# Hybrid decoder block: gates as dot products, a second broadcast of silu(c), new places for four pieces of work

## The chip, the cores and the metric

One core of a Trainium2 chip runs the whole block. The metric is the device time of one execution in microseconds (us). A run's time is a little more than the span of its trace, which goes from the first to the last instruction.

## What is computed

The reference, cut to what the change touches (x is 512 x 1024, c is one row of 1024):

```python
mod = silu(c) @ w_ada + b_ada                      # 6 sections of 1024
shift1, scale1, gate1, shift2, scale2, gate2 = split(mod, 6)
h = rms_norm(x, norm1_g) * (1 + scale1) + shift1
z = h @ w_in                                       # u, v, q, k, v, indexer, gates
merged = sigmoid(g_a) * (gmlp(z) @ w_proj_a) + sigmoid(g_b) * (sparse_attention(z) @ w_proj_b)
x = x + gate1 * (merged @ w_out)
h2 = rms_norm(x, norm2_g) * (1 + scale2) + shift2
f_g, f_u = split(h2 @ w_ffn_in, 2)
x = x + gate2 * ((silu(f_g) * f_u) @ w_ffn_out)
out = rms_norm(x, final_norm_g)
```

## The kernel before, in words

All values are float32. A large product is taken in three matmuls, hi x hi, lo x hi and hi x lo, where hi is the rounded copy of an operand and lo the rest (helper lines 107 to 109). Weights come in chunks of 512 KB over SyncE's (SP's) queue, a stream with a fixed order (`ensure`, `prep`); ScalarE (ACT) makes hi (L161), VectorE (DVE) or GpSimd (POOL) makes lo (L165). Every engine runs its instructions in the order in which the program issues them; nothing is reordered.

**The head.** The four tiles of x (128 rows each) are loaded. ACT squares each and sums (L521), POOL turns the sum into 1/rms (L404, L405), DVE or ACT scales the tile (L525, L528). c arrives as a row; TensorE (PE) spreads it over 128 partitions in PSUM, as a matmul of a row of ones with c (L517, two matmuls of 512 columns), and ACT writes silu of it to `csb` (L533). The shift and scale of the first modulation are dot products along the row: `mod_row` lets DVE multiply 128 rows of the transposed weights `w_shsc` with csb and sum them into one column of G1 (L245). Then, for each of eight blocks of 128 columns (kt), PE transposes four tiles of x (L500), ACT applies scale and shift and writes hT (L505) and a full copy (L507), DVE takes the rest (L560), and PE makes 18 matmuls into two banks of k and four of q (L568, L570, L574). While PE waits in the head it multiplies the identity with itself (`keep_warm`, L513); the result isn't read. A chain of small DVE operations prepares the rotary angles (`run_chain`, L416 to L428), some of them ahead of the scalings, some within the kt loop.

**The gates.** gate1 and gate2 are made another way: `mod_sec` multiplies 16 chunks of w_ada with single values of silu(c) and adds them up on DVE (L234), with rows spread over the partitions; `sec_tasks` then sums over the partitions by two matmuls with ones into a bank named mod (L480, L481), and DVE adds that to the bias, which POOL's queue had broadcast (L483). For gate2 this stands at the end of q = 10 in the loop described next, in banks 3 and 2.

**The FFN's first products.** They run as a loop over q = 0 to 17, by a scheme that makes a 2 x 2 block of products out of seven smaller ones: seven times `sprod` into banks R[0] to R[3], where ACT copies one bank to seed the next (L1709, L1720), and the work of the following q (`pre[0]` to `pre[3]`) is issued in between.

**The end.** The last products are added to the residual by DVE (L1266, L1268), the last partial sum of squares is taken by a dot (L1908), POOL takes the power -1/2 (L1911), and `finish` scales the columns with ACT and DVE (L1776, L1777) and stores them.

A pool's tiles of one name share `bufs` buffers; a new tile of that name waits until the readers of the one that had the buffer are done.

Of the kernel before, what the change touches and what calls it, by code (L numbers as in the profile page):

```python
# [9 lines left out]
F32 = mybir.dt.float32  # L10
# [20 lines left out]
def _plan():  # L31
# [4 lines left out]
    def pairs(*starts):  # L36
# [10 lines left out]
        "w_ada": [(2 * q, 2, ((sec * D + 512 * h, 512),)) for sec in (2, 5) for h in range(2) for q in range(4)],  # L47
# [3 lines left out]
def _pack(w, name):  # L51
    import numpy as np
    rows = w.reshape(128, 8, -1).transpose(1, 0, 2) if name == "w_ada" else w.reshape(-1, 128, w.shape[1])
# [6 lines left out]
def block_kernel(ctx: ExitStack, tc: tile.TileContext, x, w_ada, b_ada, w_in,  # L60
# [7 lines left out]
    psum = ctx.enter_context(tc.tile_pool(name="psum", bufs=1, space=bass.MemoryType.PSUM))  # L68
# [3 lines left out]
    def packed(ap, name):  # L72
        at, o = {}, 0
        for k0, nk, cols_ in _plan()[name]:
# [5 lines left out]
    w_ada, w_in, w_ffn_in, w_ffn_out = (packed(*a) for a in ((w_ada, "w_ada"), (w_in, "w_in"), (w_ffn_in, "w_ffn_in"),  # L80
                                                             (w_ffn_out, "w_ffn_out")))
# [14 lines left out]
    def bank(k, name="bank"):  # L96
        return psum.tile([128, 512], F32, name=name, tag=f"b{k}", bufs=1)
# [101 lines left out]
    cols = tiny.tile([128, 64], F32, name="cols")  # L199
    cs = cols[:, 0:8]  # L200
# [9 lines left out]
    pack = mid.tile([128, 315], F32, name="pack", tag="A2", bufs=1)  # L210
    A.dma_start(pack, small)
# [15 lines left out]

    def mac(o, w, j, first, on_act=False):
        if first and on_act:
            A.activation(o, w, AF.Copy, scale=cs[:, j:j + 1])  # L230
        elif first:
            V.tensor_scalar(o, w, cs[:, j:j + 1], None, op0=OP.mult)
        else:
            V.scalar_tensor_tensor(o, w, cs[:, j:j + 1], o, op0=OP.mult, op1=OP.add)  # L234

    def mod_row(s, kt):
        k = slice(kt, kt + 1)
        o = G1[:, s, k] if s < 2 else Gc[:, 1, 8 * (3 - s) + kt:8 * (3 - s) + kt + 1]
        scale, init = ((1.0, bsh1), (n1c[:, k], bsc1), (1.0, bsh2), (n2c[:, k], bsc2))[s]
# [9 lines left out]
    acc = {}  # L249

    def mod_sec(sec):
        for half in range(2):
            for q in range(4):
                def dma(raw, half=half, q=q):
                    SY.dma_start(raw, w_ada(2 * q, 2, ((sec * D + half * 512, 512),)))

                def fn(raw, half=half, q=q):
                    if q == 0:
                        acc[sec, half] = base.tile([128, 512], F32, name="acc", tag="acc", bufs=2)
                    v = raw.rearrange("p (j n) -> p j n", j=2)  # L260
                    for j in range(2):
                        mac(acc[sec, half], v[:, j], 2 * q + j, q == 0 and j == 0)
                    if q == 3:
                        ah = None
                        if sec == 5:
                            return
                        if sec == 2:
                            ah = t512("ah", F32R)
                            al = base.tile([128, 512], F32R, name="al", tag="acc", bufs=2)
                            V.tensor_copy(ah, acc[sec, half])  # L270
                            V.tensor_sub(al, acc[sec, half], f(ah))
                            acc[sec, half] = al
                        sec_done.append((sec, half, tick[0] + 2, ah))
                yield dma, fn
# [23 lines left out]
    def mods_mid():  # L298
        yield from mod_sec(2)
        for s in (2, 3):  # L300
            for kt in range(8):
                yield mod_row(s, kt)
# [9 lines left out]
    stream[W_GB[1][0]]["lo"] = V  # L312
    W_PB = [group(w_pb, 256 * g, mods=mm_, nm=((0, 1), (1, 1), (1, 0), (0, 0))[g], mraw="k_hi") for g in range(4)]
# [3 lines left out]
    mg = mod_sec(5)  # L317
    wh = ["E5", "E6", "E0", "E1"]
# [74 lines left out]
    mhalf = tiny.tile([128, 8], F32, name="mhalf")  # L393
    ones = mid.tile([128, 128], F32, name="ones", tag="A3", bufs=1)
    onesr = tiny.tile([128, 128], F32R, name="onesr")
    P.memset(mhalf, -0.5)
# [71 lines left out]
    def sec_tasks(flush=False, one=False):  # L468
        tick[0] += 1
        while sec_done:  # L470
            if one and one == 2:
                break
            one = one and 2
            sec, half, t, ah = sec_done[0]
            if t >= tick[0] and not flush:
                break
            sec_done.pop(0)
            a = acc[sec, half]
            p = bank(mbank[0], "mod")
# [1490 lines left out]
```

## Time and profile before

| | us |
|---|---|
| median of 3 runs | 795.21 (794.40 to 795.68) |
| the profiled execution's own time | 796.31 |
| its span | 794.5 |
| PE busy | 782.0 |
| DVE busy | 679.9 |
| ACT busy | 424.6 |
| POOL busy | 162.3 |
| mean DMA rate | 177 GB/s |

The profiled execution is a single one, so its lines are read against its own time. Busy time of matmuls is modelled at their ends; start times are not. A row of the timeline has the start, the duration, the engine, the line, and behind the operation the idle time before it with what ended it; xN groups N instructions, and the duration is then that from the first start to the last end.

### The profile page before, as it was taken

The numbers are of one execution on the slowest core, as the hardware profiler recorded it, in microseconds if no ns is written. First come the engines' busy times: TensorE is split into PE (matmuls) and PEld (weight loads), VectorE is DVE, ScalarE is ACT, GpSimd is POOL, SyncE is SP. The second block draws the span as 40 slices with busy tenths as digits, with TensorE's granted clock in tenths as the row PEclk, the third lists the DMA queues.
The fourth block names the chain that finished last, engine by engine and source line by source line (L and its number), as shares of the span: only waits on it lengthen the run. The fifth ranks groups of instructions, "written<-read, shape, count | busy, mean of one in ns | idle before, by whom it ended". The sixth has DMA issues, their size and how long they took to land.

```text
span 794.5 us, 12279 instructions
## 1 busy us (share of the span) xinstructions
PE 782.0 (98%) x4633; PEld 695.2 (88%) x4633; DVE 679.9 (86%) x1134; ACT 424.6 (53%) x753; POOL 162.3 (20%) x185
## 2 busy tenths in 40 slices
PE   7999999999999999999999999999999999999996
PEld 5889888888888888988888899999999999888885
DVE  5989788898899758887697878989999988998886
ACT  5564545323332227665636577555556666666654
POOL 3060042362344421000010010312221223000001
PEclk9999999999999999999999999999999999999999
DMA  9853352322335561137691602889896977567764
GB/s 363 333 152 119 107 185 80 123 92 90 107 134 177 207 227 66 54 106 257 203 275 35 212 28 96 249 239 292 261 266 194 255 205 200 153 192 203 225 181 146
DMA packets 40924, 140.78 MB, mean 177 GB/s; under 512 B 5025, under 2 KB 5793, under 8 KB 40866
## 3 DMA queue, kind: packets, MB, share of 16 engines
q1 hardware_dynamic: 31392, 109.82, 41.1%
q0 software_dynamic: 8752, 29.10, 14.5%
q10 hardware_dynamic: 722, 1.08, 0.4%
q8 instruction: 36, 0.59, 0.3%
q14 instruction: 22, 0.18, 0.1%
HBM read 137.63 MB, written 25.17 MB: 205 GB/s over the span
## 4 chain that ended last, share of the span: by engine, by line
PE 97%; ACT 1%; DMA 0%; issue 0%; DVE 0%; POOLq 0%; ACTq 0%; POOL 0%
PE pb L109 9%; PE pb L107 9%; PE pb L108 9%; PE R L107 8%; PE R L109 8%; PE R L108 8%; PE pfo L107 4%; PE pfo L109 4%; PE pfo L108 4%; PE pgb L107 2%; PE pgb L108 2%; PE pgb L109 2%; PE pav L109 2%; PE pav L107 2%; PE pav L108 2%; PE po L107 2%
## 5 line engine op out<-in xcount | busy, mean ns | idle before, releaser
L161 ACT ACTIVATE hi<-raw 128x1024 fp32r<-128x1024 f32 (+2 forms) x107 | 108.6, 1017 | 102.3 <-DMA raw<-in_w_proj_a_dram 23.3
L165 DVE TENSOR_TENSOR lo<-raw,hi 128x1024 fp32r<-128x1024 f32 (+2 forms) x71 | 82.8, 1169 | 20.4 <-ACT hi L161 19.9
L165 POOL TENSOR_TENSOR lo<-raw,hi 128x1024 fp32r<-128x1024 f32 x29 | 72.5, 2502 | 122.9 <-ACT hi L161 97.4
L107 PE MATMUL pb<-h,hi 128*128 128x512 f32 (+1 forms) x192 | 73.6, 383 | 0.0
L108 PE MATMUL pb<-h,hi 128*128 128x512 f32 (+1 forms) x192 | 73.0, 380 | 0.0
L109 PE MATMUL pb<-h,lo 128*128 128x512 f32 (+1 forms) x192 | 73.0, 380 | 0.0
L107 PE MATMUL pfo<-hi,za 128*128 128x512 f32 (+1 forms) x144 | 55.3, 384 | 0.0
L109 PE MATMUL pfo<-hi,za 128*128 128x512 f32 (+1 forms) x144 | 55.2, 383 | 0.0
L108 PE MATMUL pfo<-lo,za 128*128 128x512 f32 (+1 forms) x144 | 55.2, 383 | 0.0
L107 PE MATMUL R<-tb,sx 128*128 128x256 f32 x160 | 44.5, 278 | 0.6 <-ACT R L1709 0.4
L374 POOL COPY sm<-sm 128x1 f32<-128x1 f32 x36 | 23.0, 638 | 106.3 <-ACT sm L373 106.3
L107 PE MATMUL R<-tb,hi 128*128 128x256 f32 x160 | 44.3, 277 | 0.0
L108 PE MATMUL R<-tb,hi 128*128 128x256 f32 x160 | 44.3, 277 | 0.0
L109 PE MATMUL R<-tb,lo 128*128 128x256 f32 x160 | 44.3, 277 | 0.0
L109 PE MATMUL R<-tb,sx 128*128 128x256 f32 x160 | 44.2, 277 | 0.0
L108 PE MATMUL R<-tb,sx 128*128 128x256 f32 x160 | 44.2, 277 | 0.0
L109 PEld LDWEIGHTS pb<-h,lo 128*128 128x128 f32 x192 | 36.0, 188 | 6.3
L107 PEld LDWEIGHTS pb<-h,hi 128*128 128x128 f32 x192 | 36.1, 188 | 6.0
L108 PEld LDWEIGHTS pb<-h,hi 128*128 128x128 f32 x192 | 36.1, 188 | 6.0
L107 PEld LDWEIGHTS pfo<-hi,za 128*128 128x128 f32 x144 | 27.1, 188 | 5.9 <-ACT ps L1813 0.6
L109 PEld LDWEIGHTS pfo<-hi,za 128*128 128x128 f32 x144 | 27.1, 188 | 5.3
L108 PEld LDWEIGHTS pfo<-lo,za 128*128 128x128 f32 x144 | 27.1, 188 | 5.3
(388 smaller groups left out, 2568.3 us busy)
## 6 DMA issues: line engine op xcount, KB each, us to landing
raw<-in_w_ffn_in_dram SPq DMA_DIRECT2D x44, 512.0 KB, 5.5
raw<-in_w_in_dram SPq DMA_DIRECT2D x40, 512.0 KB, 3.4
wsum<-in_w_ffn_out_dram POOLq DMA_DIRECT2D x30, 512.0 KB, 8.0
raw<-wsum SPq DMA_DIRECT2D x20, 512.0 KB, 3.7
s<-in_w_shsc_dram SPq DMA_DIRECT2D x16, 512.0 KB, 7.9
mraw<-in_w_ada_dram SPq DMA_DIRECT2D x16, 512.0 KB, 3.9
raw<-in_w_ffn_out_dram SPq DMA_DIRECT2D x15, 512.0 KB, 4.3
mraw<-in_w_shsc_dram SPq DMA_DIRECT2D x11, 512.0 KB, 3.7
```

Source lines behind the costliest of these rows:

```text
L107: T.matmul(o, wh, rh, start=start, stop=False, **kw)
L108: T.matmul(o, wh, rlo, start=False, stop=False, **kw)
L109: T.matmul(o, wlo, rh, start=False, stop=stop, **kw)
L161: A.activation(hi[:, :m], e["raw"][:, :m], AF.Copy)
L165: e["lo"].tensor_sub(lo[:, :m], e["raw"][:, :m], f(hi[:, :m]))
L374: P.tensor_copy(t, t)
```

## The change

* Gates: `w_ada` and `b_ada` are no longer inputs. `w_shsc` has six sections in place of four, and gate1 and gate2 become dots on DVE as the others are, a column for 128 outputs (`Gg`). From each four columns ACT makes eight 128x128 diagonals, hi and lo (`gate_diag`, L255), and two matmuls of ones with them spread the columns as a row over the partitions (`gate_sum`, L259, L260); ACT copies the bank out (L261). For gate1 the diagonals are due two chunks behind their last dot, the matmuls two further; for gate2 the pieces are issued at the ends of q = 5, 6, 7 and 9 and of 9, 10, 11 and 13, in bank 0.
* Head: pack goes first on SP's queue, c alone on ACT's. ACT takes silu of the row of c (L401) and PE spreads it twice, into `pc` and `pc2` (L524). The first two dots read `pc` in PSUM; csb is copied from `pc2` (L545). The chain of small operations is moved ahead of the first scalings (17 steps, not 8). PE begins with nine fillers on a tile of ones (L521). The fillers, pc, pc2 and an unused tile lie in a pool of their own, `epool`, with one buffer for each name; it is closed behind the first block's h.
* FFN: `pre[1]` of the last q is issued behind the seed of R[2]; `wh` has another order; three lo chunks go from POOL to DVE.
* End: columns 512 to 768 are scaled by the gain before the last partial sum, and `finish` takes 768 to 1024 in one DVE operation, 512 to 768 in another and 0 to 512 on ACT.

```diff
-    pack = mid.tile([128, 315], F32, name="pack", tag="A2", bufs=1)
-    A.dma_start(pack, small)
+    pack = mid.tile([128, 323], F32, name="pack", tag="A2", bufs=1)
+    SY.dma_start(pack, small)
     A.dma_start(crow, c_row)
...
-            V.tensor_tensor_reduce(out=raw, in0=raw, in1=csb, scale=scale, scalar=init[:, k], op0=OP.mult, op1=OP.add,
-                                   accum_out=o)
+            V.tensor_tensor_reduce(out=raw, in0=raw, in1=csb if s > 1 or kt else pc, scale=scale, scalar=init[:, k],
+                                   op0=OP.mult, op1=OP.add, accum_out=o)
...
+    def gate_diag(o, col, half):
+        for j in range(4):
+            A.activation(o[:, j * 128:(j + 1) * 128], ident, AF.Copy, scale=col[:, 4 * half + j:4 * half + j + 1])
+
+    def gate_sum(g, half, dh, dl, b):
+        p = bank(b, "mod")
+        T.matmul(p, onesr, dh, start=True, stop=False)
+        T.matmul(p, onesr, dl, start=False, stop=True)
+        A.activation(gate_b[1 + g][:, half * 512:(half + 1) * 512], p, AF.Copy)
...
+    for i in W_AU[1] + W_AU[2][:1]:
+        stream[i]["lo"] = V
...
-    A.activation(cs, pack[:, 0:8], AF.Silu)
-    A.activation(ident, pack[:, 187:315], AF.Copy)
-    V.tensor_copy(cols[:, 8:59], pack[:, 8:59])
-    posi = pack[:, 59:187].bitcast(I32)
-
     sm = tiny.tile([128, 64], F32, name="sm")
     mhalf = tiny.tile([128, 8], F32, name="mhalf")
+    P.memset(mhalf, -0.5)
+    A.activation(sm[:, 60:61], mhalf[:, 0:1], AF.Silu)
+    A.activation(ident, pack[:, 195:323], AF.Copy)
+    A.activation(crow, crow, AF.Silu)
+    V.tensor_copy(cols[:, 0:67], pack[:, 0:67])
...
-                keep_warm(1)
+                keep_warm(3)
...
-    warm = bank(0, "warm")
+    warm = epool.tile([128, 512], F32, name="warm")
+    epool.tile([128, 512], F32, name="none1")
+    pc = epool.tile([128, D], F32, name="crow")
+    pc2 = epool.tile([128, D], F32, name="crow")
+    for k in (6, 7):
...
-    pc = [bank(2 + h, "crow") for h in range(2)]
-    for h in range(2):
-        T.matmul(pc[h], ones[0:1, :], crow[:, h * 512:(h + 1) * 512], start=True, stop=True)
-    keep_warm(16)
+    for _ in range(9):
+        T.matmul(warm[:, :128], ones, ones, start=True, stop=True)
+    for p in (pc, pc2):
+        for h in range(2):
+            T.matmul(p[:, h * 512:(h + 1) * 512], ones[0:1, :], crow[:, h * 512:(h + 1) * 512], start=True, stop=True)
...
-    norm1(0)
-    norm1(1)
-    for h in range(2):
-        A.activation(csb[:, h * 512:(h + 1) * 512], pc[h], AF.Silu)
-    norm1(2)
-    norm1(3)
-    run_chain(8)
+    for i in range(4):
+        norm1(i)
+    run_chain(17)
     scale_x(0, 0, D)
     run_chain(2)
     scale_x(1, 0, 256)
-    ensure(W1M[0])
     scale_x(2, 0, 256)
+    for h in range(2):
+        A.activation(csb[:, h * 512:(h + 1) * 512], pc2[:, h * 512:(h + 1) * 512], AF.Copy)
     act_scale(3, slice(0, 256))
     ensure(W1M[1])
     ensure(W1[0])
     pt0 = stage_T(0)
-    keep_warm(3)
+    keep_warm(5)
     stage_E(0, pt0)
+    early.close()
+    psum.append(ctx.enter_context(tc.tile_pool(name="psum", bufs=1, space=bass.MemoryType.PSUM)))
     stream[W1[0]]["do"]()
     act_scale(1, slice(256, D))
     act_scale(2, slice(256, D))
...
-        for fn in pre[1]:
-            fn()
+        if q < NQ - 1:
+            for fn in pre[1]:
+                fn()
         sprod(R[1], S2_, TB[2], False)
         wstep()
         A.activation(R[2], R[1], AF.Copy)
+        if q == NQ - 1:
+            pre[1][0]()
         pre[2][0]()
         pre[2][1]()
         sprod(R[0], A12, HB[1, 0], False)
...
-        if q == 9:
-            last_gate()
-        if q == 10:
-            for b_ in (3, 2):
-                mbank[0] = b_
-                sec_tasks(one=True)
+        if q in (5, 6, 7, 9):
+            last_gate(0, (q - 5) - q // 9)
+        if q in (9, 10, 11, 13):
+            last_gate(1, (q - 9) - q // 13)
...
-        A.activation(xo[tk][:, 640:], xo[tk][:, 640:], AF.Copy, scale=r2[:, tk:tk + 1])
-        V.tensor_scalar(xo[tk][:, :640], xo[tk][:, :640], r2[:, tk:tk + 1], None, op0=OP.mult)
-        for c, q in ((slice(0, 640), SY), (slice(640, 1024), A)):
+        r = r2[:, tk:tk + 1]
+        V.scalar_tensor_tensor(xo[tk][:, 768:], xt[tk][:, 768:], r, fng[0][:, 768:], op0=OP.mult, op1=OP.mult)
+        A.activation(xo[tk][:, :512], xo[tk][:, :512], AF.Copy, scale=r)
+        V.tensor_scalar(xo[tk][:, 512:768], xo[tk][:, 512:768], r, None, op0=OP.mult)
+        for c, q in ((slice(0, 512), A), (slice(512, 1024), SY)):
...
+                scale_g(512, n, tk)
...
-                scale_g(512, 512, tk)
```

PE in the head, from the first spread of c to the first k (x_97 to x_103 are the four tiles of x, k_228 the first bank of k). Before:

```order
L517 MATMUL crow<-crow,ones 128x512 [waits DMAHW2_49,Pool_49]
L517 MATMUL crow<-crow,ones 128x512
L513 MATMUL warm<-ident 128x128 [waits Activation_49]
L513 MATMUL warm<-ident 128x128 x15
L500 MATMUL xT<-ident,x_97 128x128 [waits DVE_49]
L500 MATMUL xT<-ident,x_99 128x128 [waits DMAHW3_49,DVE_49]
L500 MATMUL xT<-ident,x_101 128x128 [waits DMAHW4_49,DVE_49]
L513 MATMUL warm<-ident 128x128
L500 MATMUL xT<-ident,x_103 128x128 [waits DMAHW5_49,Activation_49]
L513 MATMUL warm<-ident 128x128 x3
L568 MATMUL k_228<-h_131,hi 128x512 [waits DVE_49,Activation_49]
```

And now, from the first of the four spreads on (x_103 to x_109 are the tiles of x):

```order
L524 MATMUL crow<-crow,ones 128x512 [waits Activation_49]
L524 MATMUL crow<-crow,ones 128x512
L524 MATMUL crow<-crow,ones 128x512 [waits DVE_49,PE_49]
L524 MATMUL crow<-crow,ones 128x512
L518 MATMUL warm<-ident 128x128 x6
L500 MATMUL xT<-ident,x_103 128x128
L500 MATMUL xT<-ident,x_105 128x128 [waits DMAHW3_49]
L500 MATMUL xT<-ident,x_107 128x128 [waits DMAHW4_49]
L518 MATMUL warm<-ident 128x128 x3
L500 MATMUL xT<-ident,x_109 128x128 [waits DMAHW5_49,Activation_49]
L518 MATMUL warm<-ident 128x128 x5
L574 MATMUL k_256<-h_138,hi 128x512 [waits DVE_49,PE_49,Activation_49]
```

The third matmul of L524, the first into pc2, has a wait for DVE and PE; six fillers, all transposes and k are behind it.

DVE in the head, from the last steps of the chain ahead of the scaling of x's first tile (s are rows of w_shsc, G the columns of scale and shift). Before:

```order
L424 SCALAR_TENSOR_TENSOR ropes<-ropes 128x128
L525 TENSOR_SCALAR x_97<-x_97,sm 128x1024 [waits DMAHW1_49,Activation_49,Pool_49]
L424 SCALAR_TENSOR_TENSOR ropes<-ropes 128x128 [waits DVE_49] x2
L525 TENSOR_SCALAR x_99<-x_99,sm 128x256 [waits DMAHW3_49,Activation_49,Pool_49]
L245 ISA s_105,G_89<-s_105,csb,cols 128x1024 [waits DMAHW6_49,Activation_49]
L245 ISA G_89 128x1
L525 TENSOR_SCALAR x_101<-x_101,sm 128x256 [waits DMAHW4_49,Activation_49,Pool_49]
L245 ISA s_107,G_89<-s_107,csb,cols 128x1024 [waits DMAHW7_49]
L245 ISA G_89 128x1
```

And now:

```order
L436 TENSOR_SCALAR ropes<-ropes 128x128 [waits DVE_49]
L532 TENSOR_SCALAR x_103<-x_103,sm 128x1024 [waits DMAHW2_49,Activation_49,Pool_49]
L437 TENSOR_TENSOR ropes<-ropes 128x128 [waits DVE_49]
L438 TENSOR_SCALAR ropes<-ropes 128x128 [waits DVE_49]
L532 TENSOR_SCALAR x_105<-x_105,sm 128x256 [waits DMAHW3_49,Activation_49,Pool_49]
L532 TENSOR_SCALAR x_107<-x_107,sm 128x256 [waits DMAHW4_49,Activation_49,Pool_49]
L244 ISA s_111,G_92<-s_111,crow,cols 128x1024 [waits DMAHW6_49,PE_49]
L244 ISA G_92 128x1
L244 ISA s_113,G_92<-s_113,crow,cols 128x1024 [waits DMAHW7_49]
L244 ISA G_92 128x1
```

The dots read the tile crow in PSUM in place of csb, and both stand behind the three scalings.

ACT in the last q of the FFN loop, around the seed of R (L1720 before, L1726 now; za is work of the products that follow). Before:

```order
L1700 ACTIVATE fs<-R 128x256
L1715 ACTIVATE ps<-R 128x256
L161 ACTIVATE hi<-raw 128x1024
L373 ACTIVATE sm<-cols 128x1
L1720 ACTIVATE R<-R 128x256
L1619 ACTIVATE za<-gq 128x1024
```

And now:

```order
L1705 ACTIVATE fs<-R 128x256
L1720 ACTIVATE ps<-R 128x256
L382 ACTIVATE sm<-cols 128x1
L1726 ACTIVATE R<-R 128x256
L162 ACTIVATE hi<-raw 128x1024
L1624 ACTIVATE za<-gq 128x1024
```

The chunk's hi has moved from ahead of the seed to behind it.

## Rows read from the trace of the kernel before

**Rows 1.** The page: busy time by engine, and the chain's shares by engine.
```profile
PE 782.0 (98%) x4633; PEld 695.2 (88%) x4633; DVE 679.9 (86%) x1134; ACT 424.6 (53%) x753; POOL 162.3 (20%) x185
...
PE 97%; ACT 1%; DMA 0%; issue 0%; DVE 0%; POOLq 0%; ACTq 0%; POOL 0%
```

**Rows 2.** Waits of PE: line, releaser, us in total, times, longest.
```profile
PE R L107 <- ACT R L1709: 0.4, 1, 0.4
PE k L568 <- ACT h L505: 0.2, 1, 0.2
```

**Rows 3.** Timeline, head: start us, duration us, engine, line, operation [idle before].
```profile
4.92 3.75 PE L517 MATMUL crow<-crow,ones 1*128 1x512 f32 x4 [4.92 <-DMA crow<-in_c_row_dram]
...
5.67 0.19 DVE L389 COPY cols<-pack 128x51 f32<-128x51 f32 x1 [5.67 <-DMA pack<-in_small_dram]
...
8.09 0.28 DVE L424 SCALAR_TENSOR_TENSOR ropes<-ropes 128x128 f32<-128x128 f32 x1
...
8.20 1.10 ACT L533 ACTIVATE csb<-crow 128x512 f32<-128x512 f32 x2
8.29 0.75 DVE L525 TENSOR_SCALAR x<-x,sm 128x1024 f32<-128x1024 f32 x1
...
8.60 6.64 PE L513 MATMUL warm<-ident 128*128 128x128 f32 x32
...
10.62 1.28 DVE L245 CUSTOM_DVE_ANT_0 s<-s,csb,cols 128x1024 f32<-128x1024 f32 x1 [0.50 <-DMA s<-in_w_shsc_dram]
...
14.50 0.51 ACT L528 ACTIVATE x<-x,sm 128x256 f32<-128x256 f32 x1 [2.98 <-POOL sm L405]
...
15.08 0.49 PE L500 MATMUL xT<-ident,x 128*128 128x128 f32 x3
...
15.74 0.83 PE L513 MATMUL warm<-ident 128*128 128x128 f32 x6
...
15.94 0.78 ACT L505 ACTIVATE h<-xT,G 128x512 fp32r<-128x512 f32 x1 [0.93 <-PE xT L500]
...
16.77 0.73 PE L568 MATMUL k<-h,hi 128*128 128x512 f32 x2 [0.20 <-ACT h L505]
```

**Rows 4.** Windows: us, PE busy (records) and others, PEclk, DMA; second row L513 alone.
```profile
8.60:14.50 5.90, 5.90 (x28) 5.90 (x28) 4.71 (x11) 2.89 (x6) 4.83 (x6) 1.00 1.03 418
...
14.50:15.05 0.55, 0.55 (x7) 0.55 (x5) 1.00 1.06 428
...
792.50:794.50 2.00, 0.00 (x0) 0.00 (x0) 0.00 (x0) 0.00 (x0) 0.00 (x0) 0.56 0.31 114
```

**Rows 5.** Timeline at 616 to 618, DVE and PE.
```profile
616.02 1.27 DVE L483 TENSOR_TENSOR gate2b<-gate2b,mod 128x512 f32<-128x512 f32 x2
...
616.97 0.28 PE L108 MATMUL R<-tb,sx 128*128 128x256 f32 x1
617.09 0.28 PE L109 MATMUL R<-tb,sx 128*128 128x256 f32 x1
617.81 0.38 PE L107 MATMUL R<-tb,sx 128*128 128x256 f32 x1 [0.44 <-ACT R L1709]
```

**Rows 6.** Timeline at 676 to 678, ACT and PE.
```profile
676.57 1.07 ACT L161 ACTIVATE hi<-raw 128x1024 fp32r<-128x1024 f32 x1
...
677.64 0.28 PE L109 MATMUL R<-h,sx 128*128 128x256 f32 x1
678.06 0.39 PE L107 MATMUL R<-tb,sx 128*128 128x256 f32 x1
```

**Rows 7.** Timeline of the end, POOL, PE and ACT.
```profile
786.63 0.55 POOL L1277 TENSOR_TENSOR sm<-sm,mhalf 128x1 f32<-128x1 f32 x1 [4.49 <-DVE sm L1276]
...
787.45 0.28 PE L109 MATMUL pfo<-wx,zl 128*128 128x256 f32 x1
...
789.38 0.94 POOL L1911 TENSOR_TENSOR sm<-ss,mhalf 128x1 f32<-128x1 f32 x1 [1.07 <-DVE ss L1908]
790.35 0.61 ACT L1776 ACTIVATE xo<-xo,sm 128x384 f32<-128x384 f32 x1 [1.42 <-POOL sm L1911]
```

More of the change, by code (lines that the diff above doesn't have):

```diff
@@ L52, in _pack @@
     import numpy as np
-    rows = w.reshape(128, 8, -1).transpose(1, 0, 2) if name == "w_ada" else w.reshape(-1, 128, w.shape[1])
+    rows = w.reshape(-1, 128, w.shape[1])
     return np.concatenate([
@@ L67, in block_kernel @@
     base = ctx.enter_context(tc.tile_pool(name="base", bufs=1))
-    psum = ctx.enter_context(tc.tile_pool(name="psum", bufs=1, space=bass.MemoryType.PSUM))
+    two = ctx.enter_context(tc.tile_pool(name="two", bufs=1, space=bass.MemoryType.PSUM))
+    early = ExitStack()
+    epool = early.enter_context(tc.tile_pool(name="early", bufs=1, space=bass.MemoryType.PSUM))
+    psum = []
     x, out = x[0], out[0]
@@ L96, in bank @@
     def bank(k, name="bank"):
-        return psum.tile([128, 512], F32, name=name, tag=f"b{k}", bufs=1)
+        return (two if k > 5 else psum[0]).tile([128, 512], F32, name=name, tag=f"b{k}", bufs=1)
     def f(ap):
@@ L196, in get @@
         return chunk[i]
-    cols = tiny.tile([128, 64], F32, name="cols")
-    cs = cols[:, 0:8]
+    cols = tiny.tile([128, 80], F32, name="cols")
+    bg1, bg2 = cols[:, 0:8], cols[:, 59:67]
     n1c, bsh1, bsc1 = cols[:, 8:16], cols[:, 16:24], cols[:, 24:32]
@@ new lines, in gate1_row, with fn, diag @@
+    def gate1_row(kt):
+        dma, dot = mod_row(4, kt)
+        def fn(raw):
+            dot(raw)
+            if kt % 4 == 3:
+                half = kt // 4
+                gate_cols(0, half)
+                d = []
+                def diag():
+                    d.extend(base.tile([128, 512], F32R, name="dg", tag="acc", bufs=2) for _ in range(2))
+                    gate_diag(d[0], f(gh[:, 0]), half)
+                    gate_diag(d[1], gl[:, 0], half)
+                sec_done.append((tick[0] + 2, diag))
+                sec_done.append((tick[0] + 4, lambda: gate_sum(0, half, *d, mbank[0])))
+        return dma, fn
@@ L298, in mods_mid @@
     def mods_mid():
-        yield from mod_sec(2)
+        for kt in range(8):
+            yield gate1_row(kt)
         for s in (2, 3):
@@ L466, in block_kernel, with sec_tasks @@
     gate_b = {1: base.tile([128, D], F32, name="gate1b", tag="gate", bufs=1)}
-    def sec_tasks(flush=False, one=False):
+    def sec_tasks(flush=False):
         tick[0] += 1
         while sec_done:
-            if one and one == 2:
+            if sec_done[0][0] >= tick[0] and not flush:
                 break
[L473 to L479, printed above, removed]
-            T.matmul(p, onesr, ah, start=True, stop=False)
-            T.matmul(p, onesr, a, start=False, stop=True)
-            d = gate_b[1 if sec == 2 else 2][:, half * 512:(half + 1) * 512]
-            V.tensor_add(d, d, p)
+            sec_done.pop(0)[1]()
     mbank = [7]
@@ L1562, in t_split @@
         TB[n] = (t[:, 0], t[:, 1])
-    mgl = list(mg)
+    mgl = mg
     mgr = []
@@ L1575, in last_mod, with last_gate @@
         mgl[k][1](mgr[k % 2])
-    def last_gate():
-        t = ffn[0].tile([128, 4, S], F32R, name="ahl", tag="E6", bufs=1)
-        for half in range(2):
-            ah, al = t[:, 2 * half], t[:, 2 * half + 1]
-            split(ah, al, acc[5, half])
-            acc[5, half] = al
-            sec_done.append((5, half, 0, ah))
+    gd = []
+    def last_gate(half, k):
+        if k == 0:
+            gate_cols(1, half)
+        elif k < 3:
+            gd.append(base.tile([128, 512], F32R, name="dg", tag="acc", bufs=2))
+            gate_diag(gd[-1], f(gh[:, 1]) if k == 1 else gl[:, 1], half)
+        else:
+            gate_sum(1, half, *gd[-2:], 0)
     za, zl = {}, []
@@ L1954 @@
     w_ada = _np.asarray(inputs["w_ada"])[0]
-    given["w_shsc"] = _np.concatenate([w_ada[:, 0:2048], w_ada[:, 3072:5120]], axis=1).T
+    given["w_shsc"] = _np.concatenate([w_ada[:, k * 1024:(k + 1) * 1024] for k in (0, 1, 3, 4, 2, 5)], axis=1).T
     for name in _plan():
```

68 lines of the change are left out of this document (23 added, 45 removed).

## The prediction

> **What bounds the kernel now.** I read the page first: TensorE (PE) is busy for 782.0 us of a span of 794.5, and 97% of the chain that ended last is its [rows 1]. So time can only go or come where PE stands still, and the second view, PE's waits, has little of that inside the span: 0.4 us for ScalarE's (ACT's) R seed and 0.2 us for the first h [rows 2]. The third view, the timeline, splits the span in three. The head runs until the first projection matmul k at 16.77 [rows 3]; then comes a middle without gaps but for two R seeds at 617.8 and 678.1 [rows 5, 6]; then the end behind the last matmul [rows 7]. Of the head the reader should see that nearly all PE does before 16.77 is filler (L513, 6.64 us): x is transposed when the columns of x, the two dot products and ACT's part are there. A microsecond more or less before k is a microsecond of the total, because the middle has no slack behind it.
>
> **The head, the term that decides.** The diff asks the pool `epool` (one buffer for each name) twice for a tile "crow", so pc and pc2 share one slot. In the new order PE's third crow matmul therefore waits for VectorE (DVE): the slot comes free when the last reader of pc is done, and the readers are the two dots at L244. PE works in order, and six fillers, four transposes and k are queued behind that matmul. ACT's csb copies wait for pc2, and behind them on ACT stand x3's scaling and h; x3's transpose waits for that scaling. What was side by side in the old head becomes one row.
>
> When do the dots end? From the landing of pack on, DVE has 13 small operations, which took from 5.67 to 8.09, and now ten more ahead of x0's scaling, at 0.28 each: 5.2 us. Then come the scaling of x0 (0.75), two operations (0.55), two scalings of a quarter of the columns (taken as 0.35 each) and two dots (1.28 each, taken as 1.3) [rows 3]: 9.8 us in all. With pack as late as before that gives 15.5. pack goes first on SP's queue now, ahead of the x tiles, but no row shows how early it lands; the other bound is the first dot's own weights, whose landing released it at 10.62 [rows 3], so 10.62 + 2.6 = 13.2. I take 14.2, somewhat nearer to the early end, since pack now passes ahead of the four x tiles instead of beside them.
>
> Then the row, at the pace at which PE ran in the old head. Two crow matmuls: 4.92 to 8.60, 3.68 us, so pc2 is there at 17.9. csb 1.10 (19.0), x3's scaling 0.51 (19.5) [rows 3]. PE meanwhile does its fillers. One filler is two records. In the old head 28 records fill 5.90 us, 0.21 us each; at 14.5 the pace about doubles, to seven records that touch 0.55 us [rows 4], and the six records at 15.74 are (0.83 - 0.27) / 5 = 0.11 apart [rows 3]. [...] In the old head the pace rose 9.6 us after PE's first matmul (4.92 to 14.5). Counted from the restart at 14.2 that is 23.8. So: 12 records of filler to 20.4, three transposes to 21.0, six records to 22.3, x3's transpose to 22.5, then five fillers, of which 6.2 records fit before 23.8 and 3.8 at 0.11 behind it: 24.2. h (0.78) is done at 23.4 and does not decide. **k at 24.2 instead of 16.77: +7.4 us.** The first nine fillers on `ones` and the tiny Silu that brings ACT's table early cost nothing and give nothing, for they lie ahead of the wait.
>
> Bounds: with everything behind the restart at the faster pace pc2 takes 1.84 (16.0), csb and x3 end at 17.65, the fillers and the last transpose at 18.6, h at 19.45, so k is at 19.5 (+2.7). At the slower pace throughout, the last five fillers end at 24.6 (+7.8); and a pack no earlier than before adds 1.3 to either.
>
> **The gates.** 32 multiply-adds, the two bias broadcasts on GpSimd's (POOL's) queue and four adds go; 16 rows of `w_shsc`, of the same bytes on the same SP queue, and 16 dots come. All that is DVE and DMA work beside a PE that is busy: nothing. The 32 diagonals (128x128 on ACT) are also beside PE, ACT being busy 53% of the span [rows 1]; they stand a chunk or a q ahead of the gate matmuls that need them, of which there are eight, as before. One stall goes. In q = 10 two gate sums filled the banks of R; DVE's adds (L483, 1.27) emptied them late, the R seed came late behind that, and PE's next matmul began 0.72 us after the one before, where neighbours are 0.12 apart [rows 5]. The new sums use bank 0 at the ends of q = 9 and 13, and ACT empties it: **-0.6**. If that cover is gone, an R seed waits behind ACT's eviction, and the stall is back at the same price.
>
> **The last q.** pre[1] (a hi of 1024 columns, 1.07 on ACT) stood ahead of the R seed, and PE lost 678.06 - 677.64 - 0.12 = 0.30 [rows 6]. The hi now stands behind the seed: **-0.3**. The lo parts that move from POOL to DVE and the new places of `wh` belong to buffers whose readers show no wait [rows 2]: 0.
>
> **The end.** The scaling of columns 512 to 768 leaves the last chain and takes the gap before the last partial sum, so the pow (0.94 beside a DVE operation, 0.55 alone [rows 7]) can shrink by up to 0.39. The finish is then two DVE operations of 256 columns against ACT's 512, where ACT had 384 in 0.61 [rows 7], perhaps 0.1 longer: **-0.25**, between -0.39 and +0.1.
>
> Sum: 7.4 - 0.6 - 0.3 - 0.25 = +6.25 on the profiled execution's 796.31, so 802.6. That execution was 1.10 above the median of the runs shown (795.21): **801.5 us**. No change means within 0.2%, that is 1.6 us (793.6 to 796.8).
>
> **Rivals.**
> 1. *The wait does not bind* (not slower). If pc2 could follow pc at once, its four matmuls run from about 6.0 (4.92 plus a Silu of the row, taken as csb's 1.10) to 13.4, csb ends at 14.5, x3 at 15.0, the fillers at 15.9, the last transpose at 17.2, h and k at 18.0. That is +1.25 for the head, with the other terms +0.1: 795.3. It decides if the dots end before 9.7, where pc is done. Against it: with even the early weights they end at 13.2. Chance 0.08.
> 2. *The faster pace survives the gap.* PE has the nine fillers and pc ahead of the gap, from about 1 to 10 us; if these raise the clock and it holds over some 4 us of standing still, k is at 19.5: +1.55, 796.8. For it: 9.6 us of work raised it in the old head. At the end the clock fell at some time within 6.8 us of the last matmul (787.73) [rows 4, 7], so a hold over 4 us is possible by the row. [...] By that rule this rival falls and 801.5 stands; I give it 0.10.
> 3. *The slower pace lasts longer*, to the last filler or into the first columns of k: k at 24.6, and up to 1 us lost behind it, 801.9 to 803. For it: much of the restarted work is crow matmuls of one row and transposes, and in the old head the pace rose only 5.9 us after full fillers began. The transposes at 15.08 lie 0.11 apart, so they run at the faster pace once it is there [rows 3]. [...] Chance 0.15.
> 4. *The head is shorter than the old one*, because pack, table and filler come early and everything downstream moves up; this needs k before 16 and gives under 793.6. Nothing in the new order lets x3's transpose go before pc2. Chance 0.03.
>
> **How the numbers follow.** The forecast, a serial head with the clock rising near 24, has 0.64. Rivals 1 and 4 are nearly all that lies below the range, which begins at 796.5, just below rival 2's 796.8, and ends at 804.0: 801.5 with a late pack (+1.3) and the slower pace lasting (+1.2). Within the forecast's own bounds it is 800.5 to 802.8. Faster 0.04 (rival 4 and a little of 1), same 0.12 (most of 1, half of 2), slower 0.84.
>
> **What would show it.** Right: in PE's waits a new entry of about 4 us for crow, released by DVE's dot at L244; PE standing still from about 10 to 14; csb at about 18 to 19; k at about 24; no R wait near 617 and 678 (shifted by 7); and the pow at the end near 0.55. Wrong: crow matmuls three and four right behind the first two, k before 18, or the k loop losing time afterwards because of DVE. If the total is right but k is near 17, the time has gone elsewhere and the sum was luck.

## The result, and the profile after

The changed kernel takes **806.13 us** (median of four runs, 804.78 to 806.80) against 795.42 of the kernel before in the same comparison: a ratio of 1.0135, interval 1.0117 to 1.0153, that is 10.7 us slower. The forecast was 801.5, with a range up to 804.0: right in direction, too small by 4.6 us.

The first trace of the changed kernel is that of its fastest run (804.78, span 803.0; 8.5 us above the profiled execution of before). A second trace, taken later with the same kernel (`c1` below), is a usual run: 806.43, span 804.6. The account further down uses both.

The head first, in PE's waits of the first trace (line, releaser, us in total, times, longest); these answer to [rows 2]:

```profile
PE crow L524 <- DVE G L244: 6.6, 1, 6.6
PE warm L521 <- POOL ones L407: 1.0, 1, 1.0
PE R L108 <- ACT R L1714: 0.8, 1, 0.8
```

and in its timeline, which answers to [rows 3] (the first row of L524 is the pair into pc, the second the pair into pc2):

```profile
3.06 0.20 DVE L402 COPY cols<-pack 128x67 f32<-128x67 f32 x1 [3.06 <-DMA pack<-in_small_dram]
...
4.87 1.98 PE L524 MATMUL crow<-crow,ones 1*128 1x512 f32 x4
...
10.77 1.28 DVE L244 CUSTOM_DVE_ANT_0 s<-s,crow,cols 128x1024 f32<-128x1024 f32 x1
...
11.98 1.34 DVE L244 CUSTOM_DVE_ANT_0 s<-s,crow,cols 128x1024 f32<-128x1024 f32 x1
...
13.47 3.74 PE L524 MATMUL crow<-crow,ones 1*128 1x512 f32 x4 [6.63 <-DVE G L244]
...
17.15 2.93 PE L518 MATMUL warm<-ident 128*128 128x128 f32 x12
17.25 1.08 ACT L545 ACTIVATE csb<-crow 128x512 f32<-128x512 f32 x2 [6.62 <-PE crow L524]
18.22 0.51 ACT L535 ACTIVATE x<-x,sm 128x256 f32<-128x256 f32 x1
...
21.99 0.78 ACT L505 ACTIVATE h<-xT,G 128x512 fp32r<-128x512 f32 x1 [3.26 <-PE xT L500]
...
23.18 0.71 PE L574 MATMUL k<-h,hi 128*128 128x512 f32 x2
```

The reader should see the forecast serial chain: dots, pc2, csb, x3, transposes, h and fillers, k. PE stands still for 6.6 us in front of pc2, and k begins at 23.18 where it began at 16.77 [rows 3]: +6.4 (+7.1 in the second trace, k at 23.85).

The windows of the head show the clock (us, then busy us and instructions of PE, PEld, DVE, ACT and POOL, then PEclk, DMA share and GB/s):

```profile
8.00:14.00 6.00, 0.53 (x1) 0.50 (x2) 5.42 (x14) 2.41 (x6) 2.59 (x6) 0.50 1.02 413
14.00:21.00 7.00, 7.00 (x22) 4.51 (x21) 2.08 (x3) 1.48 (x3) 0.00 (x0) 0.50 1.02 418
21.00:24.00 3.00, 2.90 (x20) 2.60 (x20) 0.53 (x1) 2.01 (x3) 0.00 (x0) 0.91 1.03 419
```

PEclk reads 0.50 from 8 to 21; in narrower windows it is 0.50 up to 21.50, 0.94 from there to 22.00 and 1.00 from 22.00 to 24.00, so it is up again just before k. The pace agrees: the pair into pc takes 1.98 us, the pair into pc2 3.74. The column alone isn't enough: in the kernel before it reads 1.00 from 8.60 to 14.50, where the records are at the slow pace (28 in 5.90 us [rows 4], 213 ns from start to start); there the spacing of equal matmuls has to be read.

Of the middle, the seam where the kernel before lost 0.72 us [rows 5] has no wait of its own any more. A new one stands four q earlier, in q = 6, on ACT and PE:

```profile
583.67 0.75 ACT L1711 ACTIVATE fs<-fs 128x256 f32<-128x256 f32 x2 [1.63 <-DVE fs L1743]
584.33 1.26 ACT L255 ACTIVATE dg<-ident,gh 128x128 fp32r<-128x128 f32 x4
585.50 0.19 ACT L382 ACTIVATE sm<-cols 128x1 f32<-128x1 f32 x1
585.59 0.36 ACT L1714 ACTIVATE R<-R 128x256 f32<-128x256 f32 x1
```

The four diagonals (1.26) stand ahead of the R seed, and PE's next matmul comes 1.07 us after the one before (584.93 to 586.00 in the timeline of PE). At the last q the gap of 0.42 [rows 6] is gone: the matmuls around the seam stand at 686.67, 686.79 and 686.90.

The end, which answers to [rows 7]:

```profile
797.99 0.56 POOL L1920 TENSOR_TENSOR sm<-ss,mhalf 128x1 f32<-128x1 f32 x1 [1.08 <-DVE ss L1917]
798.59 0.72 ACT L1784 ACTIVATE xo<-xo,sm 128x512 f32<-128x512 f32 x1 [1.05 <-POOL sm L1920]
798.59 0.49 DVE L1783 SCALAR_TENSOR_TENSOR xo<-xr,sm,fng 128x256 f32<-128x256 f32 x1 [0.68 <-POOL sm L1920]
```

The pow is at 0.56 in place of 0.94, but from the start of the finish to the last issue of a store it takes 0.14 longer, from there to the end of the span another 0.12, and from the start of PE's last matmul to the end of the span it is 6.94 us against 7.05 before (794.5 - 787.45): 0.1 gained.

What is left is in no wait. Counting PE's matmuls in stretches of 22 us in the loop of the FFN (us, PE busy and its records, PEclk, DMA share, GB/s), the kernel before has:

```profile
584.00:606.00 22.00, 22.00 (x197) 1.00 0.84 250
650.00:672.00 22.00, 22.00 (x197) 1.00 0.76 193
```

and the changed kernel, first trace:

```profile
588.00:610.00 22.00, 22.00 (x196) 1.00 0.91 255
654.00:676.00 22.00, 22.00 (x189) 1.00 0.79 229
```

The same matmuls of 256 columns, PE busy throughout, PEclk at 1.00, no row of any view with idle time, and yet 189 in place of 197: they start 118 ns apart instead of 113. That is 4% of all the time in which it lasts. The kernel before has stretches at 118 ns too (one from 501 to 522), but none behind its sums for gate2: from the last of them, at 614.2, to 676 its median spacing is 113 ns. Here one begins right at a gate sum, at 612 and again at 651; the first:

```profile
611.85 0.28 PE L110 MATMUL R<-tb,sx 128*128 128x256 f32 x1
611.97 0.39 PE L259 MATMUL mod<-dg,onesr 128*128 128x512 f32 x1
612.20 0.39 PE L260 MATMUL mod<-dg,onesr 128*128 128x512 f32 x1
612.43 0.28 PE L108 MATMUL R<-h,sa 128*128 128x256 f32 x1
612.55 0.28 PE L109 MATMUL R<-h,sa 128*128 128x256 f32 x1
```

### The profile page after: what moved, and what is told of

Read it like the earlier page. It is cut to its first block, busy times and chain, and to the rows that moved or that the text cites. A ratio compares the mean times of both kernels' runs of the same rounds, so it can differ in the third digit from the quotient of the medians.

```text
span 803.0 us, 12324 instructions
## 1 busy us (share of the span) xinstructions
PE 787.8 (98%) x4643; PEld 699.8 (87%) x4643; DVE 667.2 (83%) x1136; ACT 435.9 (54%) x788; POOL 152.2 (19%) x180
## 4 chain that ended last, share of the span: by engine, by line
PE 95%; DVE 2%; ACT 1%; DMA 1%; issue 0%; SPq 0%; POOL 0%; POOLq 0%; DVEq 0%; ACTq 0%
PE pb L110 9%; PE pb L108 9%; PE pb L109 9%; PE R L108 7%; PE R L110 7%; PE R L109 7%; PE pfo L108 4%; PE pfo L110 4%; PE pfo L109 4%; PE pgb L108 2%; PE pgb L109 2%; PE pgb L110 2%; PE pav L110 2%; PE pav L108 2%; PE pav L109 2%; PE po L108 2%
## 5 line engine op out<-in xcount | busy, mean ns | idle before, releaser
L166 DVE TENSOR_TENSOR lo<-raw,hi 128x1024 fp32r<-128x1024 f32 (+3 forms) x74 | 86.6, 1172 | 21.7 <-ACT hi L162 21.2
L166 POOL TENSOR_TENSOR lo<-raw,hi 128x1024 fp32r<-128x1024 f32 x26 | 62.3, 2396 | 133.6 <-ACT hi L162 102.2
L244 DVE CUSTOM_DVE_ANT_0 mraw<-mraw,csb,cols 128x1024 f32<-128x1024 f32 x27 | 39.5, 1463 | 18.8 <-DMA mraw<-in_w_shsc_dram 18.7
L383 POOL COPY sm<-sm 128x1 f32<-128x1 f32 x36 | 27.8, 780 | 105.9 <-ACT sm L382 105.9
```

The source lines that it names most:

```text
L166: e["lo"].tensor_sub(lo[:, :m], e["raw"][:, :m], f(hi[:, :m]))
L244: V.tensor_tensor_reduce(out=raw, in0=raw, in1=csb if s > 1 or kt else pc, scale=scale, scalar=init[:, k], op0=OP.mult, op1=OP.add, accum_ ...
L383: P.tensor_copy(t, t)
```

## The experiments

Each edit is made to the changed kernel unless another is named. Ratios are to the kernel before in the same comparison, whose median was 796.29 for a1 to a4, 796.95 for a5 to a7 and 795.54 for the rest. It was 795.42 where the changed kernel was first measured, so a difference between medians of two comparisons is good to about 1 us: by the ratios a1 to a3 lie 0.9 us further below the changed kernel than the medians below say.

### a1: pc2 in a slot of its own

```diff
-    pc2 = epool.tile([128, D], F32, name="crow")
+    pc2 = epool.tile([128, D], F32, name="crow2")
```

> The changed kernel with pc2 in a buffer of its own (name crow2), nothing else. Theory (the shared slot makes PE wait 6.6 us for the dots, and that alone sets the head): the wait for DVE at the crow matmuls is gone, matmuls three and four follow at about 6.9, k starts between 14.3 and 15.8 instead of 23.2, and the time falls by 7.4 to 8.9 us, from 806.1 to 797 to 799. Rival (the head is set by the slower pace of PE and by the 23 DVE operations ahead of the dots, so the slot matters little): k not before 18, the time above 800.5.

Measured: 797.12 us, ratio 1.0009 (0.9999 to 1.0019), 9.0 us under the changed kernel. The eight crow records run in one piece, and k starts at 14.90, before the old 16.77:

```profile
5.16 3.82 PE L524 MATMUL crow<-crow,ones 1*128 1x512 f32 x8
8.91 2.93 PE L518 MATMUL warm<-ident 128*128 128x128 f32 x12
...
14.07 0.78 ACT L505 ACTIVATE h<-xT,G 128x512 fp32r<-128x512 f32 x1 [1.34 <-DVE G L244]
...
14.90 0.73 PE L574 MATMUL k<-h,hi 128*128 128x512 f32 x2 [0.65 <-ACT h L505]
```

One name decides the head: k is 8.3 us earlier than in the first trace of the changed kernel, the rest of the head is a gain of some 2 us over the old one, and the second dot ends it (h waits for G). Yet the whole is only level with the kernel before, so some 2 us are lost further down, and these are not the head's.

### a2: the diagonals in the middle of the q

```diff
         pre[3][0]()
         pre[3][1]()
+        if q in (6, 7):
+            last_gate(0, q - 5)
+        if q in (10, 11):
+            last_gate(1, q - 9)
...
-        if q in (5, 6, 7, 9):
+        if q in (5, 9):
             last_gate(0, (q - 5) - q // 9)
-        if q in (9, 10, 11, 13):
+        if q in (9, 13):
             last_gate(1, (q - 9) - q // 13)
```

> The changed kernel with the four-diagonal pieces of gate2 (q = 6, 7, 10, 11) issued in the middle of the q, behind the copies of pre[3], instead of at its end ahead of the next R seed. Theory (the piece of 1.26 us on ACT stands ahead of the seed and PE waits 0.95 us for it at 584.9): no R wait near 585, PE's gap there at the usual 0.11, time lower by 0.9 to 1.1 us. Rival (the seed is late because DVE's adds and the dot at the same place are late, whatever ACT does): the gap stays at 0.5 us or more.

Measured: 805.25 us, ratio 1.0111 (1.0095 to 1.0127). The R wait is gone from PE's waits and the matmuls around the seam stand at 585.63, 585.75 and 585.86; ACT's timeline has the diagonals ahead of the idle time and the seed behind it:

```profile
582.76 1.26 ACT L255 ACTIVATE dg<-ident,gh 128x128 fp32r<-128x128 f32 x4
584.48 0.75 ACT L1711 ACTIVATE fs<-fs 128x256 f32<-128x256 f32 x2 [0.46 <-DVE fs L1747]
585.14 0.19 ACT L382 ACTIVATE sm<-cols 128x1 f32<-128x1 f32 x1
585.23 0.36 ACT L1714 ACTIVATE R<-R 128x256 f32<-128x256 f32 x1
```

The mechanism holds: the 1.07 us at the seam are gone, and the rival (DVE makes the seed late) falls. The whole time does not show it by itself: the medians differ by 0.9, but the intervals of the two ratios overlap.

The trace also bears on the spacing. In the first trace of the changed kernel the diagonals of q = 10 made PE late by 0.03 us (147 ns from 625.15 to the next start), and the spacing was back at 113 ns behind it. Here nothing makes PE late in q = 10, and the 118 ns last from 613 to 646. That the short stop is what ended it is not shown: in c1 below the same stop is there and the 118 ns go on.

And it bears on PEclk in the head. Windows of PE in a1, where PE has work throughout, and in a2, where it stands still from 7.2 to 14.28 (us, PE busy and its records, PEclk, DMA share, GB/s):

```profile
8.80:12.00 3.20, 3.20 (x15) 0.50 1.03 420
```

```profile
8.80:14.20 5.40, 0.00 (x0) 0.50 1.03 417
```

In both the column reads 1.00 for 5.30 to 8.60 and 0.50 from 8.80 on: the level fell at the same time with the gap and without it.

### a3: gate sums in 256 columns

```diff
-        T.matmul(p, onesr, dh, start=True, stop=False)
-        T.matmul(p, onesr, dl, start=False, stop=True)
+        for n in (slice(0, 256), slice(256, 512)):
+            T.matmul(p[:, n], onesr, dh[:, n], start=True, stop=False)
+            T.matmul(p[:, n], onesr, dl[:, n], start=False, stop=True)
```

> The changed kernel with each gate sum made by four matmuls of 256 columns instead of two of 512; the same products in the same bank. In the changed kernel's trace the 256-column matmuls are 113 ns apart before the gate sums of q = 9 and q = 13 and 118 ns apart behind them, for 13 and for 34 us, until a seam. Theory (the two 512-column matmuls among 256-column ones tip PE into the slower spacing): behind the sums the spacing stays at 113 ns, the time falls by 1.3 to 1.7 us. Rival (the spacing tips for another reason, or by chance, and any interruption does it): stretches at 118 ns begin at the sums or elsewhere as before, the time within 0.7 us of the changed kernel's.

In this form the gates' rows are not the reference's; the edit sets `start` in the bank a second time, for the second half. What is tested is the number and width of the matmuls beside the rest; a5 has sums of the same number and width with one start, in another order.

Measured: 804.06 us, ratio 1.0096 (1.0080 to 1.0112), 2.1 under the changed kernel. In the trace the spacing is back at 113 ns within 1.3 us behind each sum, so with sums of four 256-column matmuls in place of the two of 512 the 118 ns behind them (189 in 22 us in the changed kernel) are gone; why is not shown. Part of the gain is given back: PE now arrives earlier at the seed of q = 10, behind the diagonals, and its R waits are two, 1.0 us in all.

### a4: the three edits together

The diffs are those of a1, a2 and a3 (with a3's change of the gates' rows).

> The three edits together. Theory (the three losses are separate places on PE's path and add up): 806.1 less 7.4 to 8.9, less 1.0, less 1.5, that is 794.7 to 796.2, equal to the kernel before or up to 0.7 us under it. Rival (the losses overlap, or the head's gain is given back in the k loop): 797.5 or more.

Measured: 793.71 us, ratio 0.9978 (0.9961 to 0.9994). That is 1.0 us below the expected 794.7 to 796.2, and on the theory's side: the losses are separate and, within the 1 us between comparisons, add up. The gates' rows are those of a3, so a5 repeats it with the reference's.

### a5: the same with one start

The edits of a1 and a2, and in `gate_sum`, in place of its two matmuls:

```diff
+        for d in (dh, dl):
+            for n in (slice(0, 256), slice(256, 512)):
+                T.matmul(p[:, n], onesr, d[:, n], start=d is dh and n.start == 0, stop=d is dl and n.start > 0,
+                         skip_group_check=True)
```

> Two slots, the diagonals moved and the gate sums in 256 columns, now with one start for the bank and the four matmuls in the order hi, hi, lo, lo. Theory (three separate losses of the changed kernel, all undone): k at about 14.9, no seed wait near 577, the slower spacing of 118 ns gone within 2 us behind the gate sums of q = 9 and 13; time 793 to 795, that is 1 to 3 us under the kernel before. Rival (the gain of the three-fold kernel came with sums of another form and does not hold in this order): 796 or more.

Measured: 795.38 us, ratio 0.9979 (0.9963 to 0.9995), a little above the expected 793 to 795. That median lies between two groups of runs (below) and is no time of a usual run. No R wait, and 197 records again behind each sum, which answer to the 189 above:

```profile
609.00:631.00 22.00, 22.00 (x197) 1.00 0.83 258
648.00:670.00 22.00, 22.00 (x197) 1.00 0.75 206
```

But k is not at 14.9 here. It is at 18.41, because in this execution the crow matmuls take 7.19 us, not 3.82:

```profile
5.16 7.19 PE L526 MATMUL crow<-crow,ones 1*128 1x512 f32 x8
```

The time differs from execution to execution: the twelve runs lie in two groups of six, 793.4 to 794.7 and 796.1 to 797.6, some 3 us apart. a5's trace (797.27) is of the upper one. a4's, of a run at 793.71 of the kernel that differs in the form of the sums alone, has k at 14.86, and its span is 3.6 us shorter, as its k is 3.6 us earlier. One trace of each kind is all there is.

### a6: the old order of wh besides

```diff
-    wh = ["E5", "E1", "E0", "E6"]
+    wh = ["E5", "E6", "E0", "E1"]
```

> The kernel above with the order of wh as before the change (E5, E6, E0, E1). In the trace of the changed kernel the 256-column matmuls stand 118 ns apart from 486.6 to 507, where the kernel before had 113; that stretch costs 0.75 us. Theory (the new order of wh shifts the short stops in the pf products, and the stop at 486.6 tips PE into the slower spacing): the spacing is 113 ns again from the start of that stretch, time 0.7 us lower. Rival (the stop is from something else at that place, the transposes of h2 or the DMA issue): the stretch at 118 ns stays, the time is the same within 0.4 us.

Measured: 793.19 us, ratio 0.9956 (0.9938 to 0.9974), the best of all: 3.5 us under the kernel before by the ratio. Windows of PE behind the first pf products, a5 and then a6:

```profile
482.00:504.00 22.00, 22.00 (x187) 1.00 0.39 141
```

```profile
483.00:505.00 22.00, 22.00 (x194) 1.00 0.44 148
```

With the old order PE is at 113 ns again. It is so a second time, at the first R products, where the kernel before has a stretch at 118 ns as well (a5 has 172 records from 504 to 524). The kernel before and then a6:

```profile
502.00:522.00 20.00, 20.00 (x172) 1.00 1.01 275
```

```profile
505.00:525.00 20.00, 20.00 (x179) 1.00 1.02 287
```

Both traces, a5's and a6's, have the late k (18.4 and 18.6), and the spans differ by 1.3 us (795.5, 794.2). So an edit that I had priced at nothing moved as much as the seed's stall. Only the first place is a loss of the change, some 0.7 us; the second is a gain over the kernel before.

### a7: each gate sum twice

```diff
-        T.matmul(p, onesr, dh, start=True, stop=False)
-        T.matmul(p, onesr, dl, start=False, stop=True)
+        for _ in range(2):
+            T.matmul(p, onesr, dh, start=True, stop=False)
+            T.matmul(p, onesr, dl, start=False, stop=True)
```

> The changed kernel with each gate sum's pair of 512-column matmuls issued twice over (the second pair starts the bank anew and gives the same sum). The kernel before had four such matmuls in a row at 613.6, and its spacing behind them was 113 ns; the changed kernel has two in a row, and 118 ns. Theory A (the count in a row decides, four leave PE as it was): 113 ns behind the sums, so 0.9 us more for the four added pairs' columns on the whole path of gate2 and 0.9 us for gate1, less 1.6 us: within 0.5 us of the changed kernel's time. Theory B (any 512-column matmul among 256-column ones tips it): 118 ns stays, 1.6 to 2.0 us slower than the changed kernel.

Measured: 804.82 us, ratio 1.0096 (1.0071 to 1.0121), 1.3 below the changed kernel by the medians, in spite of 1.8 us of added matmuls. Windows behind the sum of q = 9 and that of q = 13:

```profile
629.00:651.00 22.00, 22.00 (x190) 1.00 0.80 237
656.00:678.00 22.00, 22.00 (x197) 1.00 0.75 213
```

Behind both sums the spacing is 113 ns, as theory A has it; in the first case it goes to 118 at 627.3, at a short late seed of q = 10, not at the sum. So at the sum the spacing went with the number in a row. Over the traces with 512-column sums, two in a row are followed by 118 ns at eight sums of eight (the changed kernel twice, a1, a2), four in a row by 113 at four of four (before, b1, a7). A short stop was followed by either spacing: behind the same seam it was 113 in the first trace (147 ns from start to start there). The time fits neither theory's number well; the trace's run was the slowest of four (807.15).

### c1: the changed kernel once more

> The changed kernel once more, for a second trace. The other kernels with its head had k at 23.7 to 24.2, its first trace 23.2. Theory (its first profiled execution drew an early head; the usual one is about 0.8 us later): k at 23.6 to 24.2 and a span of 803.5 or more; the R wait of 0.8 us at 585, the stretches at 118 ns from 486, 613 and 652 all there again. Rival (the stretches and the wait are chance): at least one of them is missing or lies elsewhere.

Measured: 806.33 us, ratio 1.0129 (1.0106 to 1.0152). k at 23.85; the R wait of 0.8 us is there, and so are the slow stretches (the one at the pf products from 480 on, not from 486). The one behind q = 9 now lasts from 613 to 647, although PE is late at q = 10 here too (145 ns from 625.95 to the next start, 147 in the first trace):

```profile
616.00:638.00 22.00, 22.00 (x189) 1.00 0.78 220
655.00:677.00 22.00, 22.00 (x189) 1.00 0.74 211
```

The stretches behind the two sums begin again at the same matmuls; the length of one differs, and the stop at q = 10, the same to 2 ns, doesn't explain it. This one ends at 647 without any stop: no two starts are more than 119 ns apart there.

### b1: the kernel before with the new order of wh alone

The diff is that of a6, the other way round, in the kernel before.

> The kernel before with nothing but the new order of wh (E5, E1, E0, E6). Theory (the order of wh alone tips PE into 118 ns at the pf products): a stretch at 118 ns in place of 113 from about 480 to 501, 0.7 to 1.3 us slower than the kernel before. Rival (it takes the rest of the change too): no such stretch, the same time within 0.4 us.

Measured: 796.41 us, ratio 1.0010 (0.9999 to 1.0022). The theory falls at the place that it names: in its trace 177 matmuls lie between 481 and 501, as many as before, and the stretch at 118 ns isn't there. But stretches at other places have moved: 179 for 172 from 502 to 522, and 169 (617 to 637) for 178 (618 to 638) behind the stall at 617, which is the same as before, 0.72 us. So the spacing in the kernel before differs with the order too, in one trace of each, and the equal time can be a sum of both signs. What puts the stretch to 486 in the changed kernel stays open.

### a8: one broadcast

The edits of a6, and:

```diff
-    pc2 = epool.tile([128, D], F32, name="crow2")
...
-        A.activation(csb[:, h * 512:(h + 1) * 512], pc2[:, h * 512:(h + 1) * 512], AF.Copy)
+        A.activation(csb[:, h * 512:(h + 1) * 512], pc[:, h * 512:(h + 1) * 512], AF.Copy)
```

with the loop over `(pc, pc2)` reduced to pc.

> Two slots, diagonals moved, narrow gate sums and the old wh, and now no second broadcast: csb is copied from pc as well, and the dots, in the order that results, wait for these copies. Theory (the second broadcast only keeps the dots from waiting for the copies, and costs two matmuls at the slower pace of PE where the clock rises late): k at 15.8 to 16.2 however PE's pace is, against 14.9 or 18.4; times without the upper group at 796 to 797, median 793 to 794.5. Rival (the dots behind the copies delay more than the head can take): k at 17 or later, median 794.5 or more.

Measured: 793.65 us, ratio 0.9974 (0.9965 to 0.9984), runs from 792.84 to 795.08, so without an upper group. The dots wait for the copies, and k is at 16.05 although PEclk read 0.50 around it in this execution (for 9 to 11 and for 12 to 17):

```profile
11.47 1.06 ACT L545 ACTIVATE csb<-crow 128x512 f32<-128x512 f32 x2
...
12.57 1.28 DVE L244 CUSTOM_DVE_ANT_0 s<-s,crow,cols 128x1024 f32<-128x1024 f32 x1 [0.94 <-ACT csb L545]
...
15.22 0.78 ACT L507 ACTIVATE h<-xT,G 128x512 fp32r<-128x512 f32 x1 [2.20 <-DVE G L244]
...
16.05 1.22 PE L574 MATMUL k<-h,hi 128*128 128x512 f32 x2 [0.26 <-ACT h L507]
```

Against this trace the second broadcast, in its own slot, buys 1.1 us of k where the pace is up early (a1, 14.90) and costs 2.4 where it comes late (a5, 18.41); that is one trace of each.

## Why the prediction was too low

The start of the same matmul in the traces of before and of c1 gives the account; the places are those of before.

| place | c1 later than before, us | step |
|---|---|---|
| first k (16.77) | 7.1 | the head |
| 470 | 7.0 | none |
| 502, first R products | 7.7 | spacing behind the pf products |
| 585 | 8.8 | diagonals ahead of the seed of q = 6 |
| 643, ahead of the sum of q = 13 | 8.9 | spacing behind q = 9: +1.3; stall at 617: -0.7; one of the two sums still to come: -0.5 |
| 682 | 10.2 | sum of q = 13: +0.5; spacing behind it: +1.3; seam at 678: -0.4 |
| last matmul (787.45) | 10.2 | none |
| end of the span | 10.1 | the end: -0.1 |

Between 585 and 682 the gate sums only change places, which adds nothing in all.

The step that failed with the most weight is the first one of the prediction, "time can only go or come where PE stands still": of the 10.1 us, 3.3 came while PE counted as busy throughout. The second is that the diagonals "stand a chunk or a q ahead of the gate matmuls that need them" and so cost nothing: 1.1. One by one:

* **The head: right, mechanism and size.** +7.4 was forecast; 6.4 and 7.1 were measured. The dots ended at 13.3 in the first trace, not at 14.2, as pack landed at 3.06; pc2, csb and x3 took the forecast 3.7, 1.1 and 0.5. The pace rose some 8 to 9 us behind the restart, not 9.6: in the first trace at 21.6, 8.1 us behind 13.47 (fillers 0.21 us apart ahead of it, 0.11 behind it), and in c1 the fillers at 22.40, 8.5 behind 13.86, are at the faster pace (ten records in 1.35 us). The wait for crow is 6.6 us and not 4, because pc was done at 6.9 already; that changes nothing, since the dots end the wait. a1 shows that the shared slot is the cause.
* **Rival 2 fell, in part.** Behind the nine fillers PE was at the higher pace, as it assumed (pc's pair in 1.98 us in the first trace, 2.12 in that of c1), but the level did not hold to pc2: PEclk is 0.50 from 8 to 14, and pc2's pair took 3.74 us. A rule by which an idle gap does this, and the rival falls, is shown by no run: the level fell between 8.60 and 8.80 in a2, with the gap, and in a1 as well, with PE at work throughout, on crow matmuls of one row. Why it fell stays open. Rival 3 fell: the pace rose ahead of k, among the last fillers.
* **Rival 1 described a kernel that was not there, but described it well:** with pc2 following pc at the lower pace, k at 18.0. a5 and a6 had 18.4 and 18.6; a1 and a4, with the pace up early, 14.9, which no rival had.
* **The gates, "they stand a chunk or a q ahead of the gate matmuls that need them": wrong.** It asked when the diagonals are needed, not what is queued behind them on ACT. In q = 6 that is the R seed, and PE lost 1.07 us, where I had 0. What is asked of an added wait has to be asked of added work ahead of others on an engine as well.
* **The gates, "-0.6": right, and yet a loss.** The stall at 617 is gone (-0.7 with the slower start behind it). But behind the old sums, four in a row, PE was at 113 ns; two in a row, at each of two places, put it to 118. That made +2.6 in c1 and +1.8 in the first trace. The prediction counted them as "eight, as before", at nothing; no term of its sum was for the spacing of matmuls, since PE counts as busy at either (22.00 of 22.00 us with 197 records and with 189).
* **wh, "0": wrong.** "Buffers whose readers show no wait" is no cover. The stretch behind the pf products cost 0.7, and a6 gained 1.3 by the old order, part of it at a place where the kernel before has a stretch too. b1 shows that the new order alone doesn't make the stretch.
* **The last q, "-0.3": right** (-0.4 with the slower start behind the seam). **The end, "-0.25": too much.** The pow gave its 0.38, and the wider pieces (0.14) and the store behind them (0.12) took most of it back: -0.1.

The sum by measured terms, for c1: 7.0 + 0.7 + 1.1 + 2.6 - 0.7 - 0.4 - 0.1 = 10.2, against the 10.1 measured; +6.25 was forecast. The miss of some 3.9 us lies in the two effects that had no term, 3.3 of spacing and 1.1 of the diagonals, less the 0.4 by which the head came short. How long a slow stretch lasts differs from one execution to the next: in the first trace the one behind q = 9 was short, and the term of 2.6 is the 1.8 above.

## What to carry to other kernels

Before a second tile of the same name is put into a pool with one buffer, ask which reader frees the slot, and what stands behind the waiting instruction: here one word cost about 9 us (a1). Work that is off the critical path has to be priced by what is queued behind it on its engine, even if its own result isn't due for long: here 1.26 us of diagonals on ACT cost PE 1.07 us. And a PE that is busy for 100% can still lose time, here 4% (189 matmuls in 22 us in place of 197): compare the count of matmuls in stretches of equal length, not only the waits.

## What the runs showed of the hardware that was not expected

* Read from the starts of matmuls in these traces: those of 256 columns, with a weight load each, ran at two spacings with PEclk at 1.00: 113 and 118 ns (197 and 189 in 22 us; the kernel before and a5 against the changed kernel). Behind two matmuls of 512 columns in a row between them the spacing was the slower one at eight sums of eight (the changed kernel twice, a1, a2); behind four in a row it was 113 at four of four (before, b1, a7), and behind four of 256 in the same bank within 1.3 us (a3). The slow stretches behind the sums lasted up to 34 us. A short stop was followed by either spacing: 147 ns at q = 10 by 113 in the first trace, 145 ns at the same matmul in c1 by 118. And a stretch ended without a stop (c1 at 647, the kernel before at 522, no two starts more than 119 ns apart). What sets the spacing is open.
* Read from the traces and the runs: the pace of the head came early or late from one execution to the next (k at 14.9 in a1 and a4, at 18.4 in a5), and the runs of a5 and a6 lie in two groups some 3 us apart (a5: 793.4 to 794.7 and 796.1 to 797.6; a6: 792.0 to 793.4 and 795.9 to 796.8). The runs of a1 show no such gap. In both traces of the changed kernel the late pair into pc2 took 3.74 and 3.75 us, with PEclk at 0.50, against 1.98 and 2.12 for the pair into pc.
